# Row statistics loaded by two transfers from ScalarE's queue, the forget gates' totals moved into the first pair's log-sum-exps, and the first FFN pair's gate products interleaved

## The chip, the cores and the metric

The kernel runs on one core of one Trainium2 chip. The time is the device time of one execution in microseconds (us); lower is better. A core has five engines, each with its own queue of instructions, worked off in order: TensorE (PE; its weight loads are shown apart as PEld), VectorE (DVE), ScalarE (ACT), GpSimd (POOL) and SyncE (SP), which here issues transfers. Transfers run on 16 DMA engines. Results of TensorE stand in PSUM, in banks that this kernel names `psp`, `pss`, `psd` and `psc`; everything else that is on chip stands in SBUF, in 128 partitions.

## The reference

Sixteen learned tokens are put in front of 512, so T = 528 tokens of width 1024 pass through two layers in float32. Layer 0 is attention with 16 heads of 64 and forget gates, layer 1 a gated linear recurrence; behind each comes a gated FFN with a causal convolution of three taps. What the change touches:

```python
def fox_attention(h, norm_g, w_in, b_f, q_gain, k_gain, w_out):
    xn = rms_norm(h, norm_g)
    q, k, v, f_logit, o_gate = jnp.split(xn @ w_in, [...], axis=-1)
    q = rms_norm(q.reshape(B, L, H, hd), q_gain) * (hd ** -0.5)
    k = rms_norm(k.reshape(B, L, H, hd), k_gain)
    log_f = jax.nn.log_sigmoid(f_logit + b_f)
    c = jnp.cumsum(log_f, axis=1).transpose(0, 2, 1)
    ...
        s = jnp.einsum('bqhd,bkhd->bhqk', q_blk, k)
        s = s + c_blk[..., None] - c[:, :, None, :]
        s = jnp.where(q_pos[:, None] >= key_pos[None, :], s, -jnp.inf)
        p = jax.nn.softmax(s, axis=-1)
    ...
    return (o * jax.nn.sigmoid(o_gate)) @ w_out

def conv_ffn(h, norm_g, w_gate, w_up, conv_w, conv_b, w_down):
    xn = rms_norm(h, norm_g)
    a = xn @ w_gate
    a = conv_b + conv_w[0] * a[t-2] + conv_w[1] * a[t-1] + conv_w[2] * a[t]
    return (jax.nn.silu(a) * (xn @ w_up)) @ w_down
```

## The kernel before, in words

Every float32 product is made of three products of a faster type: each factor is split into a high part and a low remainder (`hi`, `lo`, `xhi`, `xlo`), and hi x hi, lo x hi and hi x lo are added in one PSUM bank (L255, L258, L259 for a projection, `proj_unit`). Tokens go through in two halves of 264, the width into 8 blocks of 128 (`KT`). A weight block is loaded (L199), its high part cast on ScalarE (L200), its low part taken on VectorE (L126). In the FFNs the blocks have their own loads (L1176) and casts (L1169).

In `fox` the 16 heads go as 8 pairs through stages. `stage_a(p)` projects queries and keys, evicts each bank twice on ScalarE (L540 the square, L541 the value with its gain), sums the squares of a head with `hsel` (L549, four matmuls into four groups of 32 partitions of a bank `psd`), and copies them to `strow` (L550, ScalarE). Of `strow` only two rows of each group are of use, one a head. They are laid out as 64 partitions of 33 tokens in `am2` (the trace names it `am`) by four transfers on SyncE (L554), `et` is added (L557), a reciprocal root taken by steps on VectorE (`rsqrt`, L343 to L347), split in two (L560) and laid back into rows by two transfers (L564, `rows`). `et`, with the same layout, holds the tokens' sums of squares; four transfers at L439 fill it once from `ssr`.

`stage_n(p)` spreads each row over its head's 64 partitions by a matmul with a constant of zeros and ones (`selr` at L578, built from `sel`), multiplies, and splits into `stg`; `pack` sends that to the packed operands by six transfers (L605). `decays` adds the forget gates' sums, `cneg`, as rows to the keys (L617). `stage_l(p)` makes the log-sum-exps of a pair: scores (L751, L752, and a mask, L754), a maximum of each row (L764 on), an exponential that also sums (L119), then `lr` (L783), transposed on TensorE (L786), cast to `lrow` (L788) and sent into the packed queries (L791, L792). `stage_t(p)` attends: scores (L808, L809), a mask for the diagonal (L812), the exponential into `pt` (L119), the product with the values (L823).

`stage_f` makes the forget gates' logits. `forget` turns them into sums along the tokens, on a layout of 128 partitions (16 heads by 8 pieces) of 66 tokens: a polynomial for the logarithm on VectorE (L469 to L482), a scan within a piece (L484), each piece's total (L486, `tot`), a matmul with `C_PRE`, which sums the totals of the pieces ahead (L488), and their addition (L489 to L491), which gives `cneg`.

A loop over p from -3 to 7 weaves these stages: generators yield costs, and `weave` advances the one that is furthest behind its share. In a step the fill is `stage_v` (the values) and `stage_a(p + 3)`; beside it run `stage_n(p + 2)`, `stage_l(p + 1)`, `stage_t(p)`, and at p = -2 `stage_f`, with `forget` behind it. In this order instructions are recorded; a scheduler then sets the order of each engine's queue by dependencies and priorities, so that a change of a few lines can move others. A transfer counts up one of eight semaphores in turn, so each waits for the one eight before it.

In the FFN's `plain`, which serves the first pair of both FFNs, each of two blocks (`m`) is projected by the two token halves one after the other, each into a bank "s" (`pss`) for the first block and "p" (`psp`) for the second, and each half is evicted with its row scale (L1256) as it ends.

Of the kernel before, what the change touches and what calls it, by code (L numbers as in the profile page):

```python
# [12 lines left out]
F32 = mybir.dt.float32  # L13
# [8 lines left out]
P = 128  # L22
# [60 lines left out]
class Builder:  # L83
# [297 lines left out]
    def fox(self, ctx):  # L381
        nc, tc, a = self.nc, self.tc, self.a
        mm = nc.tensor.matmul
        full = [(0, 264), (264, 264)]
        sp = self.pool("fox1", 1, ctx=ctx)
# [17 lines left out]
        sel = s2.tile([P, T], F32, name="sel", tag="rows")[:16, : 4 * P].rearrange("p (w c) -> p w c", c=P)  # L403
# [27 lines left out]
        et = sp.tile([64, 33], F32, name="et")  # L431
# [3 lines left out]
            mm(sr[:2, :tn], self.onesd, self.ss[:, t0 : t0 + tn], start=True, stop=True)  # L435
            nc.vector.tensor_copy(ssr[:, t0 : t0 + tn], sr[:2, :tn])
        for g in range(4):
            t0, tn = full[g % 2]
            nc.sync.dma_start(et[16 * g : 16 * g + 16, :], ssr[:, t0 : t0 + tn].rearrange("r (j c) -> r j c", c=33))  # L439
        nc.vector.tensor_scalar(et, et, EPS, EPS, ALU.add, ALU.mult)  # L440
        self.spread_rs(rs, SEG0, start)
        rcol = [0, 1, 2, 3, 5]
# [2 lines left out]
        CW = T // 8  # L445
        z, e, w, u, lf = (sp.tile([P, CW], F32, name=n) for n in ("z", "e", "w", "u", "lf"))
        cneg = sp.tile([P, 2, CW], F32R, name="cneg")

        def stage_f():

# [16 lines left out]
        def forget():  # L467

            nc.vector.tensor_scalar(z, z, self.vcol(V_BF), None, ALU.add)  # L469
            nc.vector.scalar_tensor_tensor(e, z, -1.0, z, ALU.mult, ALU.max)  # L470
            self.act(e, e, AF.Exp, scale=-1.0)
            nc.vector.tensor_scalar(w, e, 2.0, None, ALU.add)
            nc.vector.reciprocal(w, w)
            nc.vector.tensor_tensor(w, w, e, ALU.mult)
            nc.vector.tensor_tensor(u, w, w, ALU.mult)
            nc.vector.tensor_scalar(lf, u, 2.0 / 15, 2.0 / 13, ALU.mult, ALU.add)
            for c in (11, 9, 7, 5, 3, 1):
                nc.vector.tensor_tensor(lf, lf, u, ALU.mult)
                nc.vector.tensor_scalar(lf, lf, 2.0 / c, None, ALU.add)
            nc.vector.tensor_tensor(lf, lf, w, ALU.mult)  # L480
            nc.vector.tensor_scalar(z, z, 0.0, None, ALU.min)
            self.sub(lf, lf, z)  # L482
            nc.vector.memset(u, 1.0)
            nc.vector.tensor_tensor_scan(w, u, lf, 0.0, ALU.mult, ALU.add)  # L484
            tot = sp.tile([P, 2], F32, name="tot")
            nc.vector.tensor_copy(tot, w[:, CW - 1 : CW].to_broadcast([P, 2]))  # L486
            psc = self.bank("c")[:, :2]
            mm(psc, self.cst[:, C_PRE : C_PRE + P], tot, start=True, stop=True)  # L488
            nc.vector.tensor_copy(tot, psc)  # L489
            nc.vector.tensor_scalar(w, w, tot[:, 0:1], None, ALU.add)  # L490
            nc.vector.tensor_copy(cneg[:, 0, :], w)  # L491
            self.sub(cneg[:, 1, :], w, cneg[:, 0, :].bitcast(F32))
# [21 lines left out]
        def stage_a(p):  # L514

            raw = {}
            sqs = []
            blocks = []
            for w_ in range(2):
                wt = self.weights(a["wqk"][p, w_], KT) if p else self.first[w_]  # L520
                banks = [self.bank(b) for b in ("pp", "cd")[w_]] if p == 0 else None
                blocks.append((wt, banks))
                if p == 0 and w_ == 1:
                    units = [
                        self.proj_unit(ps[:, :tn], [wt], self.x, t0, tn)
                        for wt, banks in blocks
                        for ps, (t0, tn) in zip(banks, full)
                    ]
                    for step in zip(*units):
                        yield sum(step)  # L530
            for w_, nm in ((0, "q"), (1, "k")):
                wt, banks = blocks[w_]
                sq = (s2 if w_ else self.sqp).tile([P, T], F32, name="sqq", tag="sqk" if w_ else "sq", bufs=2 - w_)
                rw = s2.tile([P, T], F32, name="raw" + nm, tag="raw" + nm)
                g = qg if nm == "q" else self.vcol(V_KG)
                for i, (t0, tn) in enumerate(full):
                    ps = banks[i] if banks else bank()
                    if not banks:
                        yield from self.proj_unit(ps[:, :tn], [wt], self.x, t0, tn)
                    nc.scalar.square(sq[:, t0 : t0 + tn], ps[:, :tn])  # L540
                    nc.scalar.activation(rw[:, t0 : t0 + tn], ps[:, :tn], AF.Copy, scale=g)  # L541
                sqs.append(sq)
                raw[nm] = rw

            strow = s2.tile([P, 264], F32, name="strow", tag="strow", bufs=1)
            pst = self.bank("d")
            for g in range(4):
                t0, tn = full[g % 2]
                mm(pst[32 * g : 32 * g + 32, :tn], hsel, sqs[g // 2][:, t0 : t0 + tn], start=True, stop=True)  # L549
            nc.scalar.copy(strow, pst[:, :264])  # L550
            yield 0.9
            am2 = self.tiny.tile([64, 33], F32, name="am2", tag="am2")
            for g in range(4):
                nc.sync.dma_start(  # L554
                    am2[16 * g : 16 * g + 16, :], strow[32 * g : 32 * g + 2, :].rearrange("r (j c) -> r j c", c=33)
                )
            nc.vector.tensor_tensor(am2, am2, et, ALU.add)  # L557
            y = self.rsqrt(am2, "q")
            yr = self.tiny.tile([64, 2, 33], F32R, name="yr", tag="yr")
            nc.vector.tensor_copy(yr[:, 0, :], y)  # L560
            self.sub(yr[:, 1, :], y, yr[:, 0, :].bitcast(F32))
            rows = rowbufs[p % 2]
            for x in range(2):
                nc.sync.dma_start(  # L564
                    rows[8 * x : 8 * x + 8, :].rearrange("r (j c) -> r j c", c=33).bitcast(F32),
                    yr[:, x, :].bitcast(F32),
                )
            scaled[p] = raw, rows
# [52 lines left out]

        def stage_l(p):
            if p == 0:
                decays(0)
            for d in packs[p]:
                yield from self.lse(d, s2, identb, maskq)
# [62 lines left out]
        for p in range(-3, NPAIR):  # L689
# [26 lines left out]
            while gated and p >= max(gated[0], 5 + gated[0] // 4):  # L716
                m = gated.pop(0)
# [397 lines left out]
    def ffn(self, ctx, layer, a0, o0):  # L1115
# [132 lines left out]
        def plain(j, out):  # L1248

            A, t = new_pair("A"), new_pair("t")[:, :, :n]  # L1250
            for m in range(2):
                wg = [block(a[f"gu{layer}"][2 * j + m, 0, k]) for k in range(2)]
                for t0, tn in ga:
                    ps = self.bank("sp"[m])[:, :tn]
                    yield from self.proj_unit(ps, wg, self.x, t0, tn)
                    nc.vector.tensor_tensor(A[:, m, 2 + t0 : 2 + t0 + tn], ps, self.rsb[:, t0 : t0 + tn], ALU.mult)  # L1256
                smooth(t[:, m, :], A[:, m, :], 2 * j + m)
                input_forms(2 * m)
# [124 lines left out]
def layout(x, meta_tokens, fox_norm, fox_w_in, fox_b_f, fox_q_gain, fox_k_gain, fox_w_out, hgrn_norm, hgrn_w_in,  # L1383
# [44 lines left out]
    o["lmask"] = lm  # L1428
    sel = np.zeros((16, 4, P), np.float32)
    for r in range(16):  # L1430
        sel[r, r // 2 % 4, 64 * (r % 2) : 64 * (r % 2) + 64] = 1.0
    o["sel"] = sel
    return o

# [11 lines left out]
```

## Time and profile before

| | |
|---|---|
| time, three runs | 1445.87, 1443.09, 1445.19 us; median 1445.19 us |
| the profiled execution | 1447.99 us, its span 1446.2 us |
| attention | 0 to about 380 us: TensorE busy 364.06 us, VectorE 230.42, ScalarE 206.86 |
| first FFN | to about 720 us: TensorE busy 334.53 of 340 us, VectorE 265.90, ScalarE 193.71 |
| recurrence | to about 1090 us: TensorE busy 370 of 370 us, VectorE 250.84, ScalarE 131.82 |
| second FFN | to 1446.2 us: TensorE busy 349.09 of 356.2 us, VectorE 262.20, ScalarE 191.49 |

The profile is of one execution. An instruction's row gives its start in us, its length, engine, line, operation, what it writes and reads, and in square brackets the time that the engine sat idle ahead of it, with what ended that. The names of buffers in such rows have no numbers. "SPq" marks transfers that SyncE issues; their length is that of the issue, not of the transfer. The granted clock of TensorE is given as a share of full speed.

### The profile page before, as it was taken

The numbers are of one execution on the slowest core, as the hardware profiler recorded it, in microseconds if no ns is written. First come the engines' busy times: TensorE is split into PE (matmuls) and PEld (weight loads), VectorE is DVE, ScalarE is ACT, GpSimd is POOL, SyncE is SP. The second block draws the span as 40 slices with busy tenths as digits, with TensorE's granted clock in tenths as the row PEclk, the third lists the DMA queues.
The fourth block names the chain that finished last, engine by engine and source line by source line (L and its number), as shares of the span: only waits on it lengthen the run. The fifth ranks groups of instructions, "written<-read, shape, count | busy, mean of one in ns | idle before, by whom it ended". The sixth has DMA issues, their size and how long they took to land.

```text
span 1446.2 us, 29795 instructions
## 1 busy us (share of the span) xinstructions
PE 1417.7 (98%) x11368; PEld 1336.7 (92%) x11368; DVE 1009.4 (70%) x2282; ACT 723.9 (50%) x1528; POOL 178.7 (12%) x309
## 2 busy tenths in 40 slices
PE   7999999999999999999999999999999999999998
PEld 7898878999999999999999999999999899999997
DVE  6546454776698876777776667687567887777774
ACT  5355555664566555454543323333345665555551
POOL 4000000000412222221000000000022222222100
PEclk9999999999999999999999999999999999999999
DMA  4424344422889898896321202212165899989733
GB/s 162 121 63 134 67 126 124 111 86 85 225 184 253 217 227 212 204 221 152 95 77 60 88 19 71 74 60 73 60 182 138 217 251 224 233 214 224 200 89 101
DMA packets 104311, 206.90 MB, mean 143 GB/s; under 512 B 14168, under 2 KB 18008, under 8 KB 104168
## 3 DMA queue, kind: packets, MB, share of 16 engines
q1 hardware_dynamic: 79688, 158.33, 35.5%
q0 software_dynamic: 24480, 46.67, 18.7%
q8 instruction: 89, 1.46, 0.4%
q14 instruction: 54, 0.44, 0.1%
HBM read 168.53 MB, written 2.10 MB: 118 GB/s over the span
## 4 chain that ended last, share of the span: by engine, by line
PE 92%; DMA 3%; DVE 2%; ACT 1%; SPq 1%; issue 1%; ACTq 0%; DVEq 0%
PE psp L255 7%; PE psp L258 7%; PE psp L259 7%; PE pss L255 7%; PE pss L258 7%; PE pss L259 7%; PE psp L306 6%; PE psp L1192 5%; PE psp L1194 5%; PE psp L1193 5%; PE psd L1192 3%; PE psd L1193 3%; PE psd L1194 3%; PE psc L823 2%; PE pss L981 1%; PE psc L1192 1%
## 5 line engine op out<-in xcount | busy, mean ns | idle before, releaser
L126 DVE TENSOR_TENSOR lo<-raw,hi 128x512 fp32r<-128x512 f32 (+2 forms) x322 | 253.4, 791 | 86.4 <-ACT hi L1169 46.9
L255 PE MATMUL psp<-xhi,hi 128*128 128x264 f32 (+2 forms) x784 | 227.1, 290 | 6.1 <-ACT xhi L331 6.1
L258 PE MATMUL psp<-xlo,hi 128*128 128x264 f32 (+2 forms) x784 | 225.6, 288 | 0.0
L259 PE MATMUL psp<-xhi,lo 128*128 128x264 f32 (+2 forms) x784 | 225.1, 288 | 0.0
L1169 ACT CAST hi<-raw 128x512 fp32r<-128x512 f32 (+1 forms) x232 | 139.0, 604 | 171.2 <-PE pss L258 53.9
L258 PE MATMUL pss<-room,hi 128*128 128x264 f32 (+2 forms) x532 | 169.7, 320 | 0.0
L259 PE MATMUL pss<-room,lo 128*128 128x264 f32 (+2 forms) x532 | 168.9, 320 | 0.0
L255 PE MATMUL pss<-room,hi 128*128 128x264 f32 (+2 forms) x532 | 168.3, 320 | 0.0
L255 PEld LDWEIGHTS psp<-xhi,hi 128*128 128x128 f32 x784 | 148.9, 190 | 9.3 <-ACT xhi L331 6.1
L200 ACT CAST hi<-raw 128x1024 fp32r<-128x1024 f32 (+2 forms) x86 | 83.2, 968 | 146.0 <-PE psp L258 71.5
L258 PEld LDWEIGHTS psp<-xlo,hi 128*128 128x128 f32 x784 | 148.8, 190 | 2.0 <-issue 1.9
L259 PEld LDWEIGHTS psp<-xhi,lo 128*128 128x128 f32 x784 | 148.2, 189 | 2.0 <-issue 1.9
L1192 PE MATMUL psp<-xhi,hi 128*128 128x264 f32 (+1 forms) x480 | 136.5, 284 | 3.1 <-ACT hi L1169 2.3
L1194 PE MATMUL psp<-xhi,lo 128*128 128x264 f32 (+1 forms) x480 | 136.3, 284 | 0.7 <-DVE lo L126 0.5
L1193 PE MATMUL psp<-xlo,hi 128*128 128x264 f32 (+1 forms) x480 | 135.8, 283 | 0.0
L1169 ACT CAST hi<-two 128x512 fp32r<-128x512 f32 x118 | 72.9, 619 | 83.8 <-PE psd L1193 31.7
L259 PEld LDWEIGHTS pss<-room,lo 128*128 128x128 f32 x532 | 100.1, 189 | 6.3
L258 PEld LDWEIGHTS pss<-room,hi 128*128 128x128 f32 x532 | 100.2, 188 | 5.2
L255 PEld LDWEIGHTS pss<-room,hi 128*128 128x128 f32 x532 | 99.5, 188 | 4.2
L1316 DVE TENSOR_TENSOR h<-h,pss 128x264 f32<-128x264 f32 (+2 forms) x145 | 73.5, 510 | 35.8 <-PE pss L259 35.4
L1192 PEld LDWEIGHTS psp<-xhi,hi 128*128 128x128 f32 x480 | 90.7, 189 | 6.2 <-ACT hi L1169 3.7
L1192 PE MATMUL psd<-xfhi,hi 128*128 128x264 f32 (+1 forms) x320 | 91.1, 285 | 3.2 <-ACT psd L1205 1.7
(489 smaller groups left out, 3958.9 us busy)
## 6 DMA issues: line engine op xcount, KB each, us to landing
raw<-gu SPq DMA_DIRECT2D x136, 256.0 KB
two<-gu SPq DMA_DIRECT2D x102, 256.0 KB
raw<-dn SPq DMA_DIRECT2D x80, 256.0 KB
two<-gu POOLq DMA_DIRECT2D x74, 256.0 KB, 6.4
one<-gu SPq DMA_DIRECT2D x40, 256.0 KB
two<-two POOLq DMA_DIRECT2D x40, 256.0 KB, 4.8
pk<-stg SPq DMA_DIRECT2D x30, 264.0 KB
raw<-wqk SPq DMA_DIRECT2D x14, 512.0 KB
```

Source lines behind the costliest of these rows:

```text
L126: self.nc.vector.tensor_tensor(out, x, y, ALU.subtract)
L200: nc.scalar.copy(hi, raw)
L255: ins = mm(ps, hi[:, i, :], xh, start=k == 0, stop=False)
L258: mm(ps, hi[:, i, :], xl, start=False, stop=False)
L259: mm(ps, lo[:, i, :], xh, start=False, stop=k == total - 1)
L306: mm(ps[:tn, :256], y[:, t0 : t0 + tn], w, start=n == 0, stop=n == 23)
L823: ins = mm(o, v[:, j, 2 * (p % 2) + hd, :], w[hd][0], start=j == 0, stop=j == last)
L1169: nc.scalar.copy(hi, raw)
L1192: mm(ps, hi[:, k, :], xh, start=start and k == 0, stop=False, skip_group_check=not start)
L1193: mm(ps, hi[:, k, :], xl, start=False, stop=False, skip_group_check=not start)
L1194: mm(ps, lo[:, k, :], xh, start=False, stop=k == 3, skip_group_check=not start)
L1316: nc.vector.tensor_tensor(hv, hv, ps, ALU.add)
```

## The change

There are four parts. `et` is filled from one row of `ssr` alone, and the constant `sel` is laid for the order of rows that follows. `am2` is loaded by two transfers on ScalarE's queue, one a head, each of 32 rows, in place of four on SyncE's of 16. The end of `forget`, from the matmul with the totals on, becomes a function `cumulate`, which `stage_l(0)` calls after its first yield; `tot` is allocated outside. In `plain`, the projections of both token halves advance together, a step of two width blocks each, into two banks of the same name, and both are evicted behind them.

```diff
         for g in range(4):
-            t0, tn = full[g % 2]
-            nc.sync.dma_start(et[16 * g : 16 * g + 16, :], ssr[:, t0 : t0 + tn].rearrange("r (j c) -> r j c", c=33))
+            nc.sync.dma_start(et[16 * g : 16 * g + 16, :], ssr[0:1, :].rearrange("r (j c) -> r j c", c=33))
...
+        tot = sp.tile([P, 2], F32, name="tot")
...
             nc.vector.tensor_tensor_scan(w, u, lf, 0.0, ALU.mult, ALU.add)
-            tot = sp.tile([P, 2], F32, name="tot")
             nc.vector.tensor_copy(tot, w[:, CW - 1 : CW].to_broadcast([P, 2]))
+
+        def cumulate():
+
             psc = self.bank("c")[:, :2]
             mm(psc, self.cst[:, C_PRE : C_PRE + P], tot, start=True, stop=True)
             nc.vector.tensor_copy(tot, psc)
...
             am2 = self.tiny.tile([64, 33], F32, name="am2", tag="am2")
-            for g in range(4):
-                nc.sync.dma_start(
-                    am2[16 * g : 16 * g + 16, :], strow[32 * g : 32 * g + 2, :].rearrange("r (j c) -> r j c", c=33)
-                )
+
+            four = strow.rearrange("(g r) (j c) -> g r j c", g=4, c=33)
+            for r in range(2):
+                nc.scalar.dma_start(am2[32 * r : 32 * r + 32, :], four[:, r, :, :])
             nc.vector.tensor_tensor(am2, am2, et, ALU.add)
...
             if p == 0:
+                yield 0.3
+                cumulate()
                 decays(0)
...
                 wg = [block(a[f"gu{layer}"][2 * j + m, 0, k]) for k in range(2)]
-                for t0, tn in ga:
-                    ps = self.bank("sp"[m])[:, :tn]
-                    yield from self.proj_unit(ps, wg, self.x, t0, tn)
+                banks = [self.bank("sp"[m])[:, :tn] for _, tn in ga]
+
+                units = [self.proj_unit(ps, wg, self.x, *t) for ps, t in zip(banks, ga)]
+                for costs in zip(*units):
+                    yield sum(costs)
+                for ps, (t0, tn) in zip(banks, ga):
                     nc.vector.tensor_tensor(A[:, m, 2 + t0 : 2 + t0 + tn], ps, self.rsb[:, t0 : t0 + tn], ALU.mult)
...
     for r in range(16):
-        sel[r, r // 2 % 4, 64 * (r % 2) : 64 * (r % 2) + 64] = 1.0
+        i = r // 4 % 2
+        sel[r, r % 4, 64 * i : 64 * i + 64] = 1.0
```

Three places of the queues follow, in which line numbers of the changed program are two to four higher than those of before from `cumulate` on.

SyncE's queue of before, in a step of the middle pairs, where one pair is packed (`two<-stg`) and a later pair's `am` is loaded:

```order
L792 DMA pk_248<-lrow 2x16
L605 DMA two<-stg 64x2x528 x2
L605 DMA two<-stg 64x1056
L605 DMA two<-stg 64x2x528 x2
L605 DMA two<-stg 64x1056
L554 DMA am_2328<-strow 16x1x33 x4
L199 DMA raw<-wqk 128x1024 x2
L617 DMA pk_266<-cneg 1x8x66 x2
```

ScalarE's queue of the changed program, where an early pair's sums of squares are copied; the semaphores that each instruction waits for stand in brackets (DMAHW are transfers):

```order
L542 ACTIVATE sqq<-psp 128x264 [waits PE_49]
L543 ACTIVATE rawq<-psp,qg 128x264
L552 COPY strow<-psd 128x264 [waits DMAHW6_49,DMAHW4_49,PE_49]
L558 DMA am_1085<-strow 32x1x33 [waits DMAHW7_49,Activation_49]
L558 DMA am_1085<-strow 32x1x33
L119 ACTIVATE junk,ssum<-pss,negm 16x16 [waits DVE_49,Pool_49]
L119 ACTIVATE junk,ssum<-pss,negm 128x144 [waits DVE_49]
L119 ACTIVATE junk,ssum<-pss,negm 128x272 [waits DVE_49,Activation_49]
```

The four loads left SyncE's queue, where they stood behind six packing transfers; two stand in ScalarE's now, right behind the copy that they read, and in front of the exponentials of another pair's log-sum-exps. The first waits for an older transfer too.

VectorE's queue of before, at the end of the forget gates' chain, with the second pair's addition of `et` in it:

```order
L480 TENSOR_TENSOR lf<-lf,w 128x66
L126 TENSOR_TENSOR lf<-lf,z 128x66
L557 TENSOR_TENSOR am_619<-am_619,et 64x33
L126 TENSOR_TENSOR lo<-raw,hi 128x1024
L484 SCALAR_TENSOR_TENSOR w<-u,lf 128x66
L343 TENSOR_SCALAR rqq<-am_619 64x33
L486 COPY tot<-w 128x2
L345 TENSOR_TENSOR ruq<-rqq 64x33
```

The same place of the changed program (L484 is the scan in both, which this listing prints under another operation's name):

```order
L559 TENSOR_TENSOR am_618<-am_618,et 64x33
L479 TENSOR_SCALAR lf<-lf 128x66
L483 MEMSET u 128x66
L343 TENSOR_SCALAR rqq<-am_618 64x33
L480 TENSOR_TENSOR lf<-lf,w 128x66
L345 TENSOR_TENSOR ruq<-rqq 64x33
L126 TENSOR_TENSOR lo<-raw,hi 128x1024
L126 TENSOR_TENSOR lf<-lf,z 128x66
L346 SCALAR_TENSOR_TENSOR ruq<-ruq,am_618 64x33
L126 TENSOR_TENSOR lo<-raw,hi 128x1024
L484 SCALAR_TENSOR_TENSOR w<-u,lf 128x66
L485 COPY tot<-w 128x2
```

The addition moved from behind the polynomial into its last steps, and the reciprocal root's steps are mixed with the rest of the chain.

TensorE's queue of before, at the end of the first pair's attention, from the diagonal scores on:

```order
L808 MATMUL pss<-pk_248 128x144
L809 MATMUL pss<-pk_248 128x144
L808 MATMUL pss<-pk_253 128x144
L809 MATMUL pss<-pk_253 128x144
L259 MATMUL psp<-xhi,lo 128x264
L255 MATMUL psp<-xhi,hi 128x264
L258 MATMUL psp<-xlo,hi 128x264
L259 MATMUL psp<-xhi,lo 128x264
```

The same place of the changed program, where L812 and L813 are the scores, L827 the product with the values, L790 the transposition, L755 and L756 the scores of the next log-sum-exps:

```order
L812 MATMUL pss<-pk_254 128x144
L813 MATMUL pss<-pk_254 128x144
L812 MATMUL pss<-pk_249 128x16
L813 MATMUL pss<-pk_249 128x16
L812 MATMUL pss<-pk_254 128x16
L813 MATMUL pss<-pk_254 128x16
L827 MATMUL psc<-pt,v_191 64x272 x2
L827 MATMUL psc<-pt,v_191 64x144 x2
L827 MATMUL psc<-pt,v_191 64x16 x2
L790 MATMUL pss<-identr,lr_183 128x128
L755 MATMUL pss<-pk_267 128x16
```

Behind the scores, before, stand products of a later pair's projection; in the changed program the rest of the attention follows, with no projection in it until the next pair's scores are done.

## The prediction, made before the changed kernel ran

> **What bounds the kernel now.** I read the engine totals, the chain of work that ended last and the granted clock first, to see which engine sets the end; then TensorE's waits, to see what is left to gain; then the timelines of the engines behind the three waits that the change can reach.
>
> ```profile
> span 1446.2 us, 29795 instructions
> PE 1417.7 (98%) x11368; PEld 1336.7 (92%) x11368; DVE 1009.4 (70%) x2282; ACT 723.9 (50%) x1528; POOL 178.7 (12%) x309
> PE 92%; DMA 3%; DVE 2%; ACT 1%; SPq 1%; issue 1%; ACTq 0%; DVEq 0%
> core 0: 1446.2 us, clock 0.996
> ```
>
> The span is 1446.2 us, TensorE is busy for 98% of it and carries 92% of the chain. The change alters no matrix product, so only three things can move the time: idle time of TensorE, matmuls at a lower clock, and matmuls that start late behind small waits. TensorE's waits come next (engine, line, bank, what released it, us in total, times, longest):
>
> ```profile
> PE pss L751 <- DVE lrow L788: 2.1, 2, 1.9
> PE pss L786 <- DVE rqq L347: 2.0, 1, 2.0
> PE psc L488 <- DVE tot L486: 1.6, 1, 1.6
> PE pss L255 <- ACT xhi L331: 1.5, 1, 1.5
> ```
>
> The first three lie in the attention, the last at the first FFN's start. What released them is VectorE each time, yet what VectorE itself sat waiting for is its addition at L557 (start, us, instruction, idle before it):
>
> ```profile
> 66.88 0.38 PE L488 MATMUL psc<-tot,cst 128*128 128x2 f32 x2 [1.62 <-DVE tot L486]
> 99.95 0.45 PE L751 MATMUL pss<-two 66*128 66x400 f32 x1 [1.86 <-DVE lrow L788]
> 188.06 0.45 PE L786 MATMUL pss<-identr,lr 128*128 128x128 f32 x1 [1.99 <-DVE rqq L347]
> ...
> 65.09 0.19 DVE L557 TENSOR_TENSOR am<-am,et 64x33 f32<-64x33 f32 x1 [4.33 <-DMA am<-strow]
> 98.86 0.19 DVE L557 TENSOR_TENSOR am<-am,et 64x33 f32<-64x33 f32 x1 [6.18 <-DMA am<-strow]
> 187.01 0.18 DVE L557 TENSOR_TENSOR am<-am,et 64x33 f32<-64x33 f32 x1 [1.51 <-DMA am<-strow]
> ```
>
> VectorE works in order. In front of 66.88, 99.95 and 188.06 it stood still at L557 for 4.33, 6.18 and 1.51 us, until the `am` transfers had landed, and what TensorE needed was queued behind. So the three waits have one cause, and it is a transfer. SyncE's issues and ScalarE's copies say why it is late:
>
> ```profile
> 55.15 0.38 ACT L550 COPY strow<-psd 128x264 f32<-128x264 f32 x1 [0.67 <-PE psd L549]
> 177.01 0.39 ACT L550 COPY strow<-psd 128x264 f32<-128x264 f32 x1
> ...
> 53.98 6.18 SPq L605 DMA_DIRECT2D pk<-stg  x6
> 60.25 3.64 SPq L554 DMA_DIRECT2D am<-strow  x4
> 176.11 6.10 SPq L605 DMA_DIRECT2D two<-stg  x6
> 182.32 3.50 SPq L554 DMA_DIRECT2D am<-strow  x4
> ```
>
> `strow` is ready at 55.53, but SyncE issues six packing transfers until 60.16, then the four `am` ones until 63.89; they have landed at 65.09, which is 9.56 us after the copy and 1.2 after the last issue. At 177.01 it is the same: ready at 177.40, landed at 187.01.
>
> **The change part by part.** *The `am` loads: four on SyncE become two on ScalarE.* The view of L554 gives an issue its price (min, median, max ns):
>
> ```profile
> L554 SPq DMA_DIRECT2D am<-strow x32: 610/619/1723, 31.0 to 255.0; - x32
> ```
>
> No row of before shows a transfer issued by ScalarE. Bounds: nothing from the view's side of a free queue, up to 1.72 us, the longest of these; I take the median, 0.62, as the shapes are alike. Two issues end 1.24 us after `strow`, the landing takes the 1.2 us seen above: some 2.5 us instead of 9.6. In the new order VectorE comes to the addition later than that, or with less than a microsecond to wait. I count the three waits as gone: **1.62 + 1.86 + 1.99 = 5.5 us**. What is late next at 66.88 is the rest of the forget gates' chain on VectorE; the addition stands ahead of the scan now, at a place where its data is there, and the 4.33 us that VectorE lost are more than TensorE's 1.62.
>
> The Trainium skill, page "DMA: Bandwidth & Descriptors", section "Issuing engines are not separate DMA queues", speaks against a gain here: issuing from several engines saves only the sequencer's time, "which is usually small relative to the DMA itself". In this trace it is the larger part, 4.63 + 3.73 us of issuing against 1.2 us of landing; by the page's proportion the 5.5 us would stay.
>
> *The clock behind two of the waits.* The windows below hold: us, busy us of TensorE, its weight loads, VectorE, ScalarE, GpSimd, then granted clock, share of the DMA engines, GB/s.
>
> ```profile
> 65.00:70.00 5.00, 3.38 (x28) 3.17 (x27) 4.53 (x21) 1.71 (x3) 0.00 (x0) 1.00 0.63 205
> 95.00:100.00 5.00, 3.14 (x29) 2.87 (x27) 1.03 (x7) 0.00 (x0) 0.00 (x0) 1.00 0.35 81
> 100.00:105.00 5.00, 5.00 (x28) 4.72 (x29) 3.49 (x17) 3.74 (x14) 0.00 (x0) 0.66 0.03 4
> 185.00:190.00 5.00, 3.01 (x24) 2.66 (x24) 2.65 (x17) 1.32 (x7) 0.26 (x2) 0.64 0.61 210
> 190.00:195.00 5.00, 5.00 (x30) 4.56 (x30) 4.33 (x11) 3.41 (x11) 0.00 (x0) 0.67 0.20 53
> ```
>
> From 100 to 105 us the granted clock is 0.66: 5 x 0.34 = 1.7 us of work lost. From 190 to 195 it is 5 x 0.33 = 1.65 us. From 185 to 190 the clock of 0.64 lies partly over idle time; I estimate 1.94 us of work at half speed behind 188.06, so 0.95 lost. Together **4.3 us**, and it falls away with the idle time ahead of it. No drop follows the wait of 1.62.
>
> The Trainium skill, page "TensorE: Matmul & The Clock Gate", section "Why this matters for your kernels", lets the clock fall only after some 3 us of idleness; here it falls after 1.86 us in one piece and not after 1.62. If its rule held here, the drops would have another cause and the 4.3 us would stay.
>
> *`et` from one row, the new row order, `sel`.* Four transfers before, four after, of the same bytes, and the same matmuls with other constants: 0.
>
> *The totals.* `cumulate` holds the operations that `forget` ended with. TensorE has the product with the totals at the same row of its order, the 392nd, so its later call moves nothing there: 0 (bounds: -1.62, if it is this and not the addition that frees the wait, which the 5.5 holds already; +1.62, if the wait stays).
>
> *The first pair's gate products in both FFNs.* Interleaved, TensorE has two more matmuls in front of the wait at 386.48:
>
> ```profile
> 386.48 0.39 PE L255 MATMUL pss<-xhi,hi 128*128 128x264 f32 x1 [1.52 <-ACT xhi L331]
> 386.71 0.28 PE L258 MATMUL pss<-xlo,hi 128*128 128x264 f32 x1
> 386.83 0.28 PE L259 MATMUL pss<-xhi,lo 128*128 128x264 f32 x1
> ```
>
> One starts 0.12 us after another, so **0.24 us** of 1.52 are gained; bounds 0 and 1.52. In the second FFN TensorE has no such wait: 0. The evictions of both halves now come together; the next projection has another bank, which covers them; without that cover, 0.6 us.
>
> *What is given back.* The scheduler places the projections anew. Before, the end of the third pair's attention had no projection beside it, and the first's had; after, those of the first and of the fifth have none. The price is read from these rows:
>
> ```profile
> 177.65 1.07 PE L289 MATMUL pss<-raw,one 128*32 128x256 f32 x16
> 185.07 1.00 PE L823 MATMUL psc<-pt,v 128*64 128x272 f32 x12
> 112.68 1.07 PE L289 MATMUL pss<-raw,one 128*32 128x256 f32 x16
> 126.20 1.00 PE L823 MATMUL psc<-pt,v 128*64 128x272 f32 x12
> ```
>
> Bare, the stretch takes 7.4 us. Covered, it takes 13.5, of which 58 projection matmuls at 0.12 us are 7.0 and the sums of squares and row scales some 1.0: 5.5. A bare end so costs 1.9 us. Two instead of one: **+1.9** (bounds 0 and 3.8).
>
> ScalarE's new issues stand in front of its exponentials. At 0.62 us, 16 of them are 9.9 us on an engine that is busy for 50% of the time. Where projections lie beside them, those hide it; in the two bare ends TensorE waits for the exponentials, 2 x 1.24 = **+2.4** (bounds 0 and 9.9). Each issue also waits for the transfer eight before it, mostly one of SyncE's; behind it stand the exponentials, the evictions of projections and the weight casts. I set that at 0, with 13 us as the far end (below).
>
> The two bare ends may bring a clock drop like that at 100 us: 1.7 each. I take half of one, **+0.85**; bounds 0 and 3.4.
>
> Sum: -5.5 - 4.3 - 0.24 + 1.9 + 2.4 + 0.85 = **-4.9 us**. The profiled execution took 1447.99 us, 1.8 more than its span and 2.8 more than the median; it would come to 1443.1. Against the median, 1445.19, it is **1440.3 us**.
>
> **The rivals.** (1) *Everything is given back by the bare ends*: two clock drops, 3.4, in place of the half, and 1.3 us of waits at ScalarE's queue: -4.9 + 2.55 + 1.3 = -1.0, so 1444.2. For it: VectorE's wait of 1.51 sufficed for a drop at 186 us, as the bare end came just before. Against it: no DMA wait stands in the new ends. (2) *The full gain*: ScalarE's issues hide, no drop comes, and the bare ends cost the one they replace: -10.0 + 1.9 = -8.1 and up to -10, so 1435.2 to 1437.1. For it: ScalarE idles half the time. (3) *Slower*: ScalarE stops at its issues. Each waits for an older transfer in SyncE's queue, which is held for 6.1 us by the packing rows at 53.98 and 176.11. From 1.6 us in each of eight pairs on (12.8) the gain and more is gone, for the net of the rest is -10.0 + 1.9; at 1.6 it is +4.7, so 1449.9. Against it: most of the older transfers are one stage old. (4) *The change does not do what it says*: the later totals stand at the same row for TensorE, so that part alone is worth 0. The time is that of the forecast, and this has no chance of its own.
>
> **How the numbers follow.** Forecast 0.45, the full gain 0.14, all given back 0.24, slower 0.17. The range reaches from the full gain, 1435.0, to 1449.0, into the slower case; below it I leave 0.06, above it 0.10. About 0.2%, 2.9 us, is what a measurement can tell from no change. Faster by more: most of the forecast (0.41) and the full gain, 0.55. Within: the given-back case, and the edges of its neighbours, 0.30. Slower: 0.15.
>
> **What would show it.** Right: L559's addition waits for under 1 us in the second, third and sixth pair; no wait of TensorE over 1 us near 66, 99 and 187 us; no window of a lower clock there. Wrong: a lower clock or waits for exponentials near 125 and 245 us (bare ends too cheap in my sum); rows of the `am` loads on ScalarE well over 0.62 us, or waits of ScalarE in front of them (queue); the wait at L490 as long as before (the totals). The forecast fails most easily if TensorE's drops come with the new ends.

## The result and the profile after

The changed kernel takes 1450.5 us, median of 6 runs (1448.27 to 1452.86), against 1445.0 us before (6 runs, 1443.09 to 1446.44). The ratio is 1.0038, with a 95% interval of 1.0026 to 1.0051: slower by 5.5 us, where 1440.3 was forecast and the range ended at 1449.0.

The two profiled executions hide this. That of the changed kernel took 1448.27 us, 2.2 less than its median; that of before 1447.99, 3 more than its own. So the totals of the two pages can't be set against each other; what they show is where time went in each. The page after, its first two lines:

```profile
span 1446.5 us, 29762 instructions
PE 1422.5 (98%) x11368; PEld 1337.5 (92%) x11368; DVE 1010.6 (70%) x2282; ACT 723.4 (50%) x1528; POOL 178.8 (12%) x309
```

TensorE's waits after, longest first (engine, line, bank, releaser, us in total, times, longest); those at the very start and in the FFNs are left out:

```profile
PE pss L755 <- ACT pt L119: 1.2, 1, 1.2
PE pss L812 <- ACT pt L119: 1.0, 2, 0.6
PE psp L306 <- ACT rawk L543: 0.9, 1, 0.9
...
PE pss L790 <- ACT pt L119: 0.8, 1, 0.8
```

The three waits behind VectorE are gone, and so is the wait of 1.5 us for L331. In their place stand short waits for ScalarE's exponentials (`pt`), in the attention. At the first FFN's start a wait of 0.9 us for a weight block has taken the place of the last one. Yet TensorE's busy time rose, from 1417.7 to 1422.5 us, for the same products; 2.0 us of that lie in the first 380 us. Where the attention lost time, windows of ten us show (us, TensorE busy and its matmuls, clock, DMA share, GB/s), first before, then after:

```profile
110.00:120.00 10.00, 10.00 (x76) 1.00 0.59 162
120.00:130.00 10.00, 9.78 (x83) 1.00 0.69 162
180.00:190.00 10.00, 7.55 (x46) 0.82 0.79 217
240.00:250.00 10.00, 10.00 (x69) 1.00 0.74 226
```

```profile
110.00:120.00 10.00, 8.30 (x56) 0.91 0.92 242
120.00:130.00 10.00, 10.00 (x65) 0.75 0.36 117
180.00:190.00 10.00, 10.00 (x69) 1.00 0.58 180
240.00:250.00 10.00, 9.62 (x60) 1.00 0.66 189
320.00:330.00 10.00, 9.33 (x67) 1.00 0.08 26
```

The third pair's end, at 180 us, gained 23 matmuls. The first pair's end, from 110 to 130 us, lost 38, and the fifth's, at 240, lost 9; from 320 us there are 67, where before has 82. The count in the brackets is worth more here than the busy time, which stays near 10 while matmuls start late one behind the other. The prediction took the fifth pair's end to be as bare as the first's. It isn't throughout: products of a projection stand from 248.91 us on, ahead of its last products with the values at 254.60.

A second way to see it is to count products from the start. Both kernels do the same 2488 products through the part of the attention whose order e5 and e6 (below) hold, and up to the counts that follow their orders differ by at most seven of them. The 760th product starts at 109.99 us before and at 105.75 after, the 1040th at 146.05 and 148.71, the 1650th at 227.48 and 226.68, the 2488th at 332.74 and 336.99. So the changed kernel was 4.2 us ahead when the first pair's end came, lost 6.9 in and behind it, regained 3.5 around the third's, and lost 5.1 from there on, at the fifth pair's end and behind it. These are single executions: e2 below, which has the order of before, starts its 2488th at 335.00.

In windows of five us the clock after shows the same kind of drop as before had, at another place:

```profile
115.00:120.00 5.00, 4.18 (x25) 0.83 0.90 265
120.00:125.00 5.00, 5.00 (x26) 0.50 0.35 110
```

That is 5 x 0.17 + 5 x 0.5 = 3.4 us, against the 4.3 that I had counted as gone.

The loads themselves came sooner, but not as I had it. The same addition on VectorE, in the second, third and sixth pair, and two of the copies and issues in front of it:

```profile
60.60 0.19 DVE L559 TENSOR_TENSOR am<-am,et 64x33 f32<-64x33 f32 x1 [1.77 <-DMA am<-strow]
88.19 0.19 DVE L559 TENSOR_TENSOR am<-am,et 64x33 f32<-64x33 f32 x1 [3.54 <-DMA am<-strow]
176.99 0.19 DVE L559 TENSOR_TENSOR am<-am,et 64x33 f32<-64x33 f32 x1 [2.45 <-DMA am<-strow]
...
55.11 0.38 ACT L552 COPY strow<-psd 128x264 f32<-128x264 f32 x1 [0.70 <-PE psd L551]
55.52 1.66 ACTq L558 DMA_DIRECT2D am<-strow  x2
81.60 0.38 ACT L552 COPY strow<-psd 128x264 f32<-128x264 f32 x1
82.00 1.20 ACTq L558 DMA_DIRECT2D am<-strow  x2
```

From the end of the copy at 55.49 to the addition are 5.1 us, from 81.98 they are 6.2. The issues end at 57.18 and 83.20: what takes long now is the landing, 3.4 and 5.0 us, not 1.2.

### The profile page after: what moved, and what is told of

Read it like the earlier page. It is cut to its first block, busy times and chain, and to the rows that moved or that the text cites. A ratio compares the mean times of both kernels' runs of the same rounds, so it can differ in the third digit from the quotient of the medians.

```text
span 1446.5 us, 29762 instructions
## 1 busy us (share of the span) xinstructions
PE 1422.5 (98%) x11368; PEld 1337.5 (92%) x11368; DVE 1010.6 (70%) x2282; ACT 723.4 (50%) x1528; POOL 178.8 (12%) x309
## 5 line engine op out<-in xcount | busy, mean ns | idle before, releaser
L255 PEld LDWEIGHTS psp<-xhi,hi 128*128 128x128 f32 x784 | 149.2, 191 | 12.2 <-ACT xhi L331 6.2
L126 DVE TENSOR_TENSOR lo<-two,hi 128x512 fp32r<-128x512 f32 x118 | 81.1, 688 | 16.4 <-ACT hi L1173 13.5
```

The costliest lines, as they stand in the source:

```text
L126: self.nc.vector.tensor_tensor(out, x, y, ALU.subtract)
L255: ins = mm(ps, hi[:, i, :], xh, start=k == 0, stop=False)
```

## The experiments

Each was timed beside the kernel before, on the same chip; the ratios are to it, and so are differences in us (its medians lay between 1444.46 and 1444.84 us). In kernels with a held order, all products of TensorE have one line, that of the function that records them (L155 or L158), and lines are higher by some 80.

| run | kernel | us, median | ratio, 95% interval |
|---|---|---|---|
| e1 | changed, FFN as before | 1449.84 | 1.0034 [1.0024, 1.0044] |
| e2 | before, FFN interleaved | 1444.73 | 0.9996 [0.9986, 1.0006] |
| e3 | before, new rows, SyncE loads | 1446.65 | 1.0013 [1.0004, 1.0023] |
| e4 | before, four loads on ScalarE | 1448.62 | 1.0022 [1.0011, 1.0033] |
| e5 | changed, order of before | 1443.88 | 0.9991 [0.9976, 1.0005] |
| e6 | before, order of the changed | 1481.2 | 1.0248 [1.0230, 1.0267] |
| e7 | before, new rows, ScalarE loads | 1452.14 | 1.0051 [1.0035, 1.0066] |
| e8 | before, new rows, GpSimd loads | 1458.54 | 1.0101 [1.0083, 1.0118] |
| e9 | changed, new order, then old | 1448.91 | 1.0029 [1.0018, 1.0041] |
| e10 | changed, old order, then new | 1456.11 | 1.0087 [1.0064, 1.0110] |
| e11 | before, packing behind loads | 1462.53 | 1.0128 [1.0111, 1.0144] |
| e12 | the same, two loads | 1451.59 | 1.0052 [1.0034, 1.0070] |
| e13 | changed, weights ahead thrice | 1451.63 | 1.0045 [1.0029, 1.0062] |
| e14 | before, weights ahead thrice | 1442.8 | 0.9984 [0.9972, 0.9997] |
| e15 | e7, weights ahead thrice | 1443.33 | 0.9994 [0.9983, 1.0005] |
| e16 | changed, weights ahead once | 1448.02 | 1.0025 [1.0012, 1.0037] |
| e17 | changed, weights ahead twice | 1448.55 | 1.0031 [1.0019, 1.0044] |

### Which part carries the loss: e1 to e4, e7, e8

e1 is the changed kernel without this edit, e2 the kernel before with it:

```diff
-                for t0, tn in ga:
-                    ps = self.bank("sp"[m])[:, :tn]
-                    yield from self.proj_unit(ps, wg, self.x, t0, tn)
+                banks = [self.bank("sp"[m])[:, :tn] for _, tn in ga]
+                units = [self.proj_unit(ps, wg, self.x, *t) for ps, t in zip(banks, ga)]
+                for costs in zip(*units):
+                    yield sum(costs)
+                for ps, (t0, tn) in zip(banks, ga):
```

> The changed kernel without the interleaving of the first FFN pair: rows, loads on ScalarE and the later totals alone. Its order on TensorE through the attention is that of the changed kernel, with the ends of the first and the fifth pair bare. Theory A (the new order's bare ends, with a clock drop in the first, cost more than the waits gave): all of the loss is here, 1450.5, +4.5 to +6.5 us on before. Rival B (the interleaved FFN products cost it): -4 to +1 us, as the three waits are gone and nothing else is paid.

> Before with the interleaved gate products of the first FFN pair alone. Theory A: -2 to +0.5 us, nothing in the attention moves; the profiles of before and after differ by -2.9 us behind the attention, and this would show how much of it is real. Rival B: +4 to +7 us.

e1 gave +5.4 us, e2 +0.3 with an interval across none. The loss lies in the attention, and the FFN part is worth nothing that can be measured. e2 has the attention of before, and its profile is a second look at it. Two of the three waits are there, the third isn't:

```profile
PE pss L786 <- DVE rqq L347: 2.0, 1, 2.0
PE psc L488 <- DVE tot L486: 1.6, 1, 1.6
```

So the wait of 1.86 us at 99.95, and the clock drop behind it, came in only one of these two executions.

e3, e7 and e8 take `et`, `sel` and the two loads of 32 rows into the kernel before, and differ in the queue; e4 keeps the four loads of 16 rows and changes the queue alone.

```diff
-                nc.sync.dma_start(am2[16 * g : 16 * g + 16, :], ...)
+                nc.scalar.dma_start(am2[16 * g : 16 * g + 16, :], ...)   # e4
...
+                nc.sync.dma_start(am2[32 * r : 32 * r + 32, :], four[:, r, :, :])    # e3
+                nc.scalar.dma_start(am2[32 * r : 32 * r + 32, :], four[:, r, :, :])  # e7
+                nc.gpsimd.dma_start(am2[32 * r : 32 * r + 32, :], four[:, r, :, :])  # e8
```

> Before with the new rows (et, sel, two loads of 32 rows a pair) but the loads issued by SyncE as before. In its order the end of the first pair's attention stays covered by projections, that of the third is bare, that of the fifth is covered. Theory A: no loss, -3 to +1 us: two issues less, 1.2 us, in each of the three waits, whose sum shrinks from 5.5 to about 2. Rival C (ScalarE's issues cost, wherever the projections stand): the same, since ScalarE issues none. If the new rows themselves cost: over +3 us.

> Before with the four loads a pair issued by ScalarE, in the old rows: 32 issues there, twice as many as in the changed kernel. In its order the end of the first pair's attention stays covered, that of the third is bare as before. Theory A: the waits of 1.6, 1.9 and 2.0 us and the drops behind them go, the bare end of the third pair stays: -6 to 0 us. Rival C (the issues in front of ScalarE's exponentials cost): twice the issues of the changed kernel, so +5 us or more.

> Before with the new rows and ScalarE's two loads a pair alone, without the later totals and the interleaved FFN. The ends of the first and the fifth pair are bare as in the changed kernel. Theory A: +4 to +6 us, since the later totals move no product at these ends. Rival D (the later totals have a share): under +2.5 us.

> Before with the new rows and the two loads a pair issued by GpSimd, which idles through the attention: neither behind SyncE's packing nor in front of ScalarE's exponentials. The scheduler gives it an order of its own, with the first pair's end covered and the third's and fifth's bare in part. Theory A: it goes by these ends, +0 to +4 us. Rival C: no issue on ScalarE and no wait behind the packing, so -5 to -1 us.

They came out at +2.2, +4.2, +7.4 and +13.8 us, all four above what theory A had for them: no placing of the loads was free. e3 has no issue on ScalarE and is still slower; e4 has twice as many as the changed kernel and is less slow than e7. So the number of issues on ScalarE doesn't set the time. What all four share is that the scheduler set a new order for all engines.

### The order or the loads: e5, e6

Both kernels have the same products. In e5 the changed kernel gets TensorE's order of before through the attention, in e6 the kernel before gets that of the changed one. A table holds the order, as runs of recorded products, and each product is told to come behind the one ahead of it; the scheduler orders the other engines itself.

```diff
+    def hold(self):
+        last = None
+        for first, count in ORDER:
+            for i in range(first, first + count):
+                if last is not None:
+                    self.after(self.products[i], self.products[last])
+                last = i
```

> The changed kernel, whole, with TensorE's order through the attention held to that of before (each product is told to come behind the one ahead of it in that order). ScalarE issues the loads, the ends of the first and the fifth pair are covered again. Theory A (the new order on TensorE is what costs): the loss is gone, 1440 to 1445.5, -4 to +1 us on before. Rival C (ScalarE's issues and what stands behind them cost): the loss stays, 1448.5 to 1451.

> Before, with its four loads a pair on SyncE, and TensorE's order through the attention held to that of the changed kernel. Theory A: slower without any of the change's parts but the order, +4 to +8 us, 1448.5 to 1452.5. Rival C: as before, 1443.5 to 1446.

e5 gave 1443.88 us: the loss of the changed kernel, 6.6 us, is gone with all of its loads on ScalarE in place. That decides between theory A and rival C: the loss goes with TensorE's new order. What ScalarE's issues cost isn't told apart from what the sooner loads gain; the two together, with the totals and the FFN part, come to -0.9 us (interval -3.5 to +0.7). e6 was far worse than either had it. Its waits of TensorE say why:

```profile
PE psd L158 <- DMA rows<-yr: 18.9, 6, 7.0
```

With the old loads the row scales come later than the new order wants them, six times. An order fits the transfers that it was made for; in e6 it isn't the bare ends that are priced.

e5 also says why so little was gained. Its waits in the attention, and the addition ahead of the longest:

```profile
PE pss L155 <- DVE ruq L428: 2.3, 1, 2.3
```

```profile
121.83 0.19 DVE L642 TENSOR_TENSOR am<-am,et 64x33 f32<-64x33 f32 x1 [4.13 <-DMA am<-strow]
```

The wait that the change was to take away came back in the fourth pair: VectorE stood still for 4.13 us, since the loads, issued by ScalarE until 116.43, landed 5.4 us later.

### Parts of the order: e9, e10

The same table, the first 1040 products by one order and the others by the other.

> The changed kernel with TensorE's order held: the first 1040 products of the attention in the new order (through the first pair's end), the others in that of before (the fifth pair's end covered). Theory A, if the loss is in the bare ends alike: about half of the 6.6 us between the changed kernel (1450.5) and the changed kernel in the old order (1443.9), so 1446 to 1448.5. If the first pair's end with its clock drop holds it all: 1449.5 to 1451.5. If it lies elsewhere: 1443.5 to 1445.

> The counterpart: the first 1040 products in the old order, the others in the new one (the fifth pair's end bare). Theory A: the other half, 1446 to 1448.5, and the losses of this and its counterpart add up to 5 to 8 us over 1443.9.

e9 is 5.0 us over e5, between what was expected for half of the loss and for all of it; e10 is 12.2 over, outside its range. They do not add up to the 6.6 between e5 and the changed kernel, so the parts of an order aren't independent. Both are made of two halves that no scheduler put together, so e10 says nothing of the fifth pair's end, and e9's 5.0 us are an indication, not a price, for the new order up to behind the first pair's end. The profiles agree with it: from the 760th to the 1040th product e5 takes 38.1 us, e9 42.9 and the changed kernel 43.0.

### What holds the loads: e11, e12

On the kernel before, its order held to itself, the packing of a pair comes behind the next pair's loads on SyncE; e12 has the new rows with two loads.

```diff
+        for p, ins in self.packing:
+            if p + 1 in self.loads:
+                self.after(ins, self.loads[p + 1])
```

> Before, with TensorE's order held to its own and one thing changed: on SyncE the six packing transfers of a pair come behind the four loads of the next pair's rows instead of ahead of them. Theory E (the packing's 1.6 MB on the DMA engines hold the loads back, whichever queue issues them; ScalarE's queue took only the issuing away): the addition follows the copy by under 4 us in every pair, against 9.6 before and 5 to 6 with ScalarE's loads, the three waits go, -5 to -1 us. Rival F (the packing is late then, and the scores wait for it): +1 us or more. Rival G (the queue ahead of the loads was all that held them): the same as with ScalarE's loads in the old order, -2 to 0.

> The same with the new rows: two loads a pair on SyncE, ahead of the packing, TensorE's order held to that of before. The packing is 1.2 us less late than with four loads. Theory E: as e11 or up to 1.5 us less, -6 to -1 us on before. Rival F: half as late as e11, 0 to +2 us.

The mechanism of theory E held in e12, its gain did not. In e12 the second pair's copy, issue and addition, SyncE's packing behind them:

```profile
56.51 0.38 ACT L635 COPY strow<-psd 128x264 f32<-128x264 f32 x1 [0.75 <-PE psd L155]
...
56.91 1.18 SPq L641 DMA_DIRECT2D am<-strow  x2
58.15 2.09 SPq L690 DMA_DIRECT2D pk<-stg  x3
...
59.33 0.18 DVE L642 TENSOR_TENSOR am<-am,et 64x33 f32<-64x33 f32 x1
```

With no packing on the DMA engines the loads are there 1.2 us after their issue, and the addition follows the copy by 2.4 us, as I had reckoned for ScalarE's queue. With the packing in flight they take 2.9 to 5.4 in e5 and the changed kernel. It isn't ScalarE's queue that makes them slow: in the changed kernel the first pair's loads, for which no packing is under way (the DMA share from 33 to 35 us is 0.03), are issued by ScalarE too and land 1.2 us later:

```profile
31.69 1.69 ACTq L558 DMA_DIRECT2D am<-strow  x2
34.62 0.19 DVE L559 TENSOR_TENSOR am<-am,et 64x33 f32<-64x33 f32 x1 [2.47 <-DMA am<-strow]
```

But in e11 and e12 the packing is late. e11's waits:

```profile
PE pss L155 <- DMA pk<-stg: 7.7, 3, 2.7
...
PE psp L155 <- ACT hi L286: 5.0, 1, 5.0
```

Rival F: the scores wait for packed operands, and 5.0 us for a weight block. e11 came out at +17.8 us, e12 at +6.9, in place of -5 to -1.

### Why the ends are bare: e13 to e17

The profiles of before and after show SyncE's issues at the first pair's end, the weights of the next projections (`wqk`) among them, and the cast that waits for these. Before:

```profile
113.38 0.81 SPq L199 DMA_DIRECT2D raw<-wqk  x2
115.27 5.49 SPq L605 DMA_DIRECT2D pk<-stg  x5
...
117.04 1.04 ACT L200 CAST hi<-raw 128x1024 fp32r<-128x1024 f32 x1 [0.62 <-DMA raw<-wqk]
```

After:

```profile
107.71 6.18 SPq L607 DMA_DIRECT2D pk<-stg  x6
113.99 2.52 SPq L199 DMA_DIRECT2D raw<-wqk  x2
...
119.93 1.04 ACT L200 CAST hi<-raw 128x1024 fp32r<-128x1024 f32 x1 [0.91 <-DMA raw<-wqk]
```

```profile
109.96 1.07 PE L289 MATMUL pss<-raw,one 128*32 128x256 f32 x16
```

Before, the weights were issued 0.7 us behind the start of L289 (112.68), ahead of the packing, and cast 4.4 us behind it. After, with the four loads gone from SyncE and the stage earlier, the packing stands first in the queue, the weights behind it, 4.0 us behind L289, and their cast came 10 us behind it. Until then there is no projection of these weights to lay beside the end. That the missing loads are why the scheduler put the packing first is argued, not shown. These runs put the weights ahead of the packing, for the third pair (e16), the third and fifth (e17), and these and the seventh (e13 to e15), and leave all orders to the scheduler.

```diff
+            for p, ins in b.packing:
+                if p in (2, 4, 6):
+                    b.after(ins, b.ahead[p])
```

> The changed kernel with one thing added: on SyncE the packing transfers of the third, fifth and seventh pair come behind the weight loads that the projections beside the next attention need; nothing else is held, the scheduler sets every order. Theory H (the ends are bare because ScalarE's loads let SyncE reach the packing earlier, and the weights then queue behind it): the projections are back beside the ends, the loss goes, 1442 to 1446, 4 to 8 us under the changed kernel. Rival J (the order of the products costs for another reason, or the packing behind the weights makes the scores wait): 1448 or more.

> The same hold in the kernel before, its loads on SyncE unchanged. There only the third pair's end had its weights behind the packing (issued at 185.93 behind 176.11); its cover comes back, but the fifth pair's end gets less of one. Theory H: -3 to +2 us on before. Rival J: +3 us or more, as the packing and the row loads behind it come later.

> The new rows on ScalarE alone (1452.1 in e7) with the same hold. Theory H: the loss goes here too, 1443 to 1447. Rival J: 1449 or more.

> The changed kernel with the hold for the third pair's packing alone, the one in the first pair's end. Theory H: the first end's projections come back and nothing new waits at the fifth, where e13 had a wait of 3.1 us for a weight block: 1444 to 1448, 2.5 to 6.5 us under the changed kernel. Rival J: 1449.5 or more.

> The changed kernel with the hold for the third and the fifth pair's packing, not the seventh's. If the seventh's hold (the gate weights behind another pair's log-sum-exp rows) spoiled e13: 1443 to 1448. If the fifth's did: as e13, 1450 to 1453, with e16 faster.

e15 is 8.8 us under e7, from which it differs by the hold alone, and the cast stands where theory H wants it, 4.4 us behind L289's products (110.55 there):

```profile
111.25 0.81 SPq L200 DMA_DIRECT2D raw<-wqk  x2
112.15 7.08 SPq L609 DMA_DIRECT2D pk<-stg  x6
...
114.97 1.05 ACT L201 CAST hi<-raw 128x1024 fp32r<-128x1024 f32 x1 [0.71 <-DMA raw<-wqk]
```

Some 3 us of that show in the granted clock, whose mean over the runs is 0.9942 in e7 and 0.9963 in e15. On the whole changed kernel the hold gained nothing (e13, in rival J's range). Its profile has new waits instead:

```profile
PE psp L256 <- ACT hi L201: 3.6, 2, 3.1
PE psd L556 <- ACT sqq L547: 2.3, 1, 2.3
...
PE psc L832 <- ACT pt L120: 1.9, 1, 1.9
```

Without the seventh pair's hold (e16, e17) it came to 1448.0 and 1448.6 us, 2.5 and 2 under the changed kernel, though the intervals of the ratios overlap with its own; e16 is at the edge of theory H's range, e17 outside both of its ranges. In the profiles of e13, e16 and e17 the first pair's end is better (44, 40 and 40 matmuls from 120 to 125 us, against 26), but from 235 to 250 us there are 77, 55 and 81 matmuls, against 99: the hold moved much of the loss to the fifth pair's end.

So putting the weights ahead of the packing regains 8.8 us in one kernel, and at most a part of the loss in the changed one. As the hold also gives each kernel a new order, that it acts by the weights' place alone is argued, not shown. What makes up the rest of the 6.6 us stays open. e14, the kernel before with the hold, is the only version that beat the kernel before by more than the measurement leaves open, by 2 us of 1444.8 (0.9984, 0.9972 to 0.9997). Its mean clock is 0.9968, against 0.9950 of before beside it, which is worth 2.6 us, as much as the whole gain.

## Why the prediction was wrong

**The steps that failed** are two, and the larger is the gain. The prediction counted 5.5 us for the three waits, 4.3 for the clock behind them and 0.24 for the FFN, 10.0 in all. e5 has every part of the change in TensorE's old order, in which the first and the fifth pair's ends are covered, so that the terms of the bare ends fall away. It gained 0.9 us; its interval ends at 3.5. The gain was set 9.1 us too high, at least 6.5. What became of it stands below, under the three waits and the clock.

The second is "What is given back". It priced the two bare ends at 1.9 us more than before, ScalarE's issues in them at 2.4 and clock drops at 0.85, in sum 5.15. The changed kernel lies 6.6 us over e5, which is what the new order costs with the same loads: 1.5 more. The two misses make up the 10.4 us between -4.9 and +5.5, but for 0.2 by which the medians of before differ. This split holds for the timed runs. By the two profiled executions alone, in which the changed kernel was 4.2 us ahead at its 760th product, the gain would seem to have come; but that of before took 3 us more than its median, and the gain was read from it.

The bare ends were sized too small. I compared one bare end with one covered end by the time from first to last row, 7.4 us against 5.5. After, the first pair's end, bare, takes 8.3 us between the same two rows, L289 at 109.96 (above) and this one:

```profile
118.29 1.79 PE L827 MATMUL psc<-pt,v 128*64 128x272 f32 x12
```

The windows of the first and the fifth pair's end hold 56 and 60 matmuls in 10 us. Against the 77 and 73 of e5, where both are covered, that is 21 and 13 fewer; at 0.12 us each, an estimate, since matmuls differ in length, it is 2.5 and 1.6 us. Against the 84 of a full stretch (90 to 100 us in e5) it would be 3.4 and 2.9.

```profile
90.00:100.00 10.00, 10.00 (x84) 1.00 0.16 34
110.00:120.00 10.00, 10.00 (x77) 1.00 1.02 262
...
240.00:250.00 10.00, 10.00 (x73) 1.00 0.72 184
```

I followed the loads only where they went, to ScalarE's queue, not what moves up where they left: on SyncE the packing came ahead of the weight loads. I saw that the ends were bare in the new order and did not ask why; e15 suggests that a part of the reason lies in that queue. The signs that I had named told it: a lower clock near 125 us, and VectorE waiting 1.77, 3.54 and 2.45 us at L559 where under 1 was forecast.

**The three waits** of TensorE went from the places named, as forecast. Their size was one execution's: e2 shows 3.6 of the 5.5 us for the same attention. A new wait of 2.3 us, in e5, stands behind the same kind of load. And the price of the new loads was wrong. The landing of 1.2 us was read from SyncE's loads, which had just let the packing's issues by; issued beside the packing they land in 2.9 to 5.4 us, e12 shows 1.2 without it. VectorE's standing at the addition fell from 23.9 to 14.5 us, not to nothing.

The Trainium skill's "DMA: Bandwidth & Descriptors", section "Issuing engines are not separate DMA queues", which I had set aside, states first that transfers run on the same 16 DMA engines and interleave, whichever engine started them. That is what the traces show: ScalarE's loads land 2.9 to 5.4 us after their issue beside SyncE's packing, 1.2 without it. Its second sentence, that only the sequencer's time is saved, fits too: for the second pair the time from the copy to the end of the issues fell from 8.4 to 1.7 us, the landing rose from 1.2 to 3.4, and the whole fell from 9.6 to 5.1.

**The clock.** 4.3 us were counted as gained. The changed kernel lost 3.4 at another place. In e2, with the attention of before, the wait at L488 was 1.64 us, as good as the 1.62 of before that no drop followed, and this time one did:

```profile
65.00:70.00 5.00, 3.36 (x28) 1.00 0.35 122
70.00:75.00 5.00, 5.00 (x31) 0.66 0.31 106
```

And the drop of before near 188 us, 2.6 of the 4.3, was there when the wait of 1.99 us, which runs from 186.07, had hardly begun: the window from 186 to 187 us already shows 0.72. In e5 that wait is gone, no wait from 180 to 190 us is over 0.54, and the drop comes all the same, at the third pair's bare end. Before, then e5:

```profile
186.00:187.00 1.00, 0.07 (x4) 0.72 0.30 31
```

```profile
180.00:185.00 5.00, 3.59 (x29) 0.91 0.98 282
185.00:190.00 5.00, 5.00 (x23) 0.50 0.17 43
```

So a drop can't be put down to the length of one wait, and taking that wait away doesn't pay its price back for sure. Over all timed runs the granted clock hardly moved: its mean is 0.9957 in the six of the changed kernel and 0.9950 to 0.9955 in the five sets of before. That is about 1 us of gain at most, where the sum had 3.45 (4.3 less 0.85), and the slower time doesn't come from the clock.

**The totals** did as priced for TensorE: L490 starts at 65.1 us with no wait. Whether they are worth 0 in time isn't settled: e1, with them, is 2.3 us under e7, without, but the intervals of the two ratios meet.

**The FFN part**, 0.24 us: e2 can't tell it from nothing.

**The rivals.** By its number the slower one is nearest, 1449.9 at 1.6 us a pair, but by luck: its mechanism, ScalarE stopped at its issues, would have stayed in e5, where the loss is gone. By its mechanism the first is nearest, everything given back by the bare ends. It stopped at 1444.2, since it too took the full gain and had too small a price for the ends.

## What to carry to other kernels

When a load leaves a queue, ask what moves up in its place and what that now stands ahead of, not only where the load goes. If a scheduler sets the orders, time the edit with the old order held as well: that tells what the edit does from what the new order does, and here it was -0.9 us, which the measurement can't tell from none, against +6.6. And a wait read from one profiled execution should be found in a second one before its gain is counted in full.

## What was unexpected in the hardware

A half clock came after with no long idle time ahead of it. The longest wait of TensorE near it is 1.16 us; the clock fell in the window from 115 us, in which TensorE was busy for 4.18 of 5 us but started only 25 matmuls, behind 110 to 115 with 4.12 busy. The page "TensorE: Matmul & The Clock Gate" of the Trainium skill, section "Why this matters for your kernels", speaks of some 3 us of idleness; in these traces a stretch of ten us with 56 matmuls in place of 84 had a drop in it, and e5 had one with no wait over 0.54 us near it, so the page's rule and the traces differ.
